# Ten instead of nine of the first table's sixteen column blocks on TensorE, and gathered rows of 768 instead of 896 columns

## The chip, the cores and the metric

The kernel runs on one core of one Trainium2 chip. The metric is the time of one execution on the device, in microseconds (us). Engines are named as in the profile: PE is TensorE's matmul side and PEld its weight load, DVE is VectorE, ACT is ScalarE, POOL is GpSimd and SP is SyncE, whose queue issues the plain loads here. The profile's source lines (L1879 and so on) are lines of the kernel file.

## What is computed

One layer of a decoder: an input projection, a recurrent (RWKV-7) and a sparse-attention mixer, an output projection, a layer norm, and then an expert mixer (PEER) with a second norm, for 256 prompt tokens and 32 sample tokens. The change concerns the expert mixer of the prompt tokens alone. Each token chooses 128 of 16384 experts (8 heads, 16 each). An expert e is a row of the first table, u, and a row of the second table, v, both 2048 wide:

```python
q = (xt @ wq).reshape(n, P_HEADS, 2, P_DKEY // 2)
s = jnp.einsum('nhcd,hckd->nhck', q, subkeys).astype(jnp.float32)
hv, hix = lax.top_k(s, P_TOPK)
...
tv, tpos = lax.top_k(cand, P_TOPK)
expert = jnp.take_along_axis(cand_e, tpos, axis=-1)
gate = jax.nn.softmax(tv, axis=-1).astype(x.dtype)
...
h = jax.nn.gelu(jnp.einsum('cd,chkd->chk', xb, u_tab[eb]), approximate=False)
return jnp.einsum('chk,chkd->cd', gb * h, v_tab[eb])
```

## The kernel before

**Two ways to one dot product.** For each token and chosen expert the kernel needs the dot product of the token with the expert's row of u, 2048 columns long, which is 16 column blocks of 128. The columns are split. The last NDB = 9 column blocks are computed densely on TensorE, for all 16384 experts and all 256 tokens, whether chosen or not. The first 7 blocks, UG = 896 columns, are computed sparsely: for one of a token's 128 choices, GpSimd gathers the 128 rows that 128 tokens chose (an indirect DMA of 128 x 896 floats, `gather` at L457), and VectorE multiplies them with the tokens and adds along the row (`dot`, L1803). There are 2 token tiles x 128 choices, so 256 such dots. Each writes one column of HD, and tile 0's 128 come first.

**The dense stage.** A loop over i1 from 0 to 127 (L1892) calls `dense` (L1874), which treats the 128 experts of one block:
- L1876 loads `ur`, 128 x 1152 floats (576 KB), over SP's queue into one of NUR = 3 buffers.
- L1879 multiplies the last three of the nine columns (NSP to NDB) in float32; such a matmul shows as two passes, so six passes a block. Xfd holds the tokens' part.
- The other NSP = 6 columns go in two halves, SPLIT = ((0, 3), (3, 6)). For a half, ACT casts the weights to f32r (`uh`, L1639), DVE subtracts the cast from the weights (`ul`, L1640), both in the helper `columns`, and PE makes three products a column: uh with XHd, uh with XLd, ul with XHd (L1886), nine passes a half, eighteen a block. uh and ul have three buffers each.
- L1888: ACT copies the block's sums from the PSUM bank `ph` (five banks) to AW, a store of all 16384 sums of each of 256 tokens.

After each block the loop puts ND or ND + 1 dots into VectorE's stream, by the rule `n_ = ND + (i1 * NDN % 8 < NDN)`: with ND = 1 and NDN = 4 it is 2, 1, 2, 1, so 1.5 a block. The gathers have a ring of NRW = 5 row buffers. Some dots already stand between the last selections ahead of the stage (the lines to L1431, with the helpers of `choose` and `settle`), beside the first blocks of `dense`. When tile 0's dots are done, `table(0)` (L1810) turns indices, gates and HD into TB.

**The weigh stage.** A loop over 68 steps (L1995 on) treats four tokens a step. `pick` (L1918) writes one-hot tables `oo` of the chosen indices on VectorE, PE transposes them (L1922, `pt`), ACT copies them (L1924, `oT`); PE multiplies them with AW (L1930, `px`); VectorE multiplies that with the other half of the one-hots and sums (L1941, `xj`, into E), which picks the dense sums of the chosen experts; then come the activation, the gate (L1949), the scaling (L1955) and a product that puts the weights back into AW (L1963, `pa`). These instructions are kept in the written order. The dots that are not done yet, `left` of them, are spread over the first 28 steps. From step 28 on the sample tokens' products follow (L1982, `fs`). `ws` (L1971) is one VectorE operation ahead of the loop.

**What sets the order.** The compiler's scheduler sorts the instructions of each engine by priorities; `tc.high_priority` lifts the casts and subtractions of the first NPRI = 12 blocks, and `issue_after` keeps an instruction behind another. On the chip each engine then takes its rows strictly in that order.

Behind the weigh stage the second table's products (L2058 and L2085) follow. The host arrays `in_peer_u_t` (dense part) and `in_peer_u_g` (gathered part) are cut by NDB and UG.

Of the kernel before, what the change touches and what calls it, by code (L numbers as in the profile page):

```python
# [11 lines left out]
F32R = mybir.dt.float32r  # L12
# [6 lines left out]
P = 128  # L19
# [30 lines left out]
NDW = 1  # L50
NPRI = 12
ND = 1
NDN = 4
NUR = 3
NRW = 5
NDB = 9
SPLIT = ((0, 3), (3, 6))
NSP = SPLIT[-1][1]
UG = 128 * (16 - NDB)
WF = 3  # L60
# [92 lines left out]
def hybrid_decode_step(ctx: ExitStack, tc: tile.TileContext, a, outs, dbg=None):  # L153
# [37 lines left out]
    def bank(tag="pb"):  # L191
        places = [(pool, nm, n) for _, div in psum for t_, pool, nm, n in div for _ in range(n) if t_ == tag]
        turn[tag] = k = (turn.get(tag, -1) + 1) % len(places)
        pool, nm, n = places[k]
        return pool.tile([P, 512], F32, name=tag, tag=nm, bufs=n)
# [1441 lines left out]
    def columns(pb, xh, xl):  # L1637

        sc.copy(xh, pb)  # L1639
        return ve.tensor_tensor(xl, pb, xh.bitcast(F32), OP.subtract)  # L1640
# [138 lines left out]
    dp, kc, kq = (Pool(nm, "left") for nm in ("dp", "kc", "kq"))  # L1779
    dp([P, NDB, P], "ur", bufs=NUR)  # L1780
    XHd, XLd = dp([P, NSP, NPR], "XHd", F32R), dp([P, NSP, NPR], "XLd", F32R)
    Xfd = dp([P, NDB - NSP, NPR], "Xfd")
    SKT = kq([P, 16, P], "SKT")
# [75 lines left out]
    for q in range(NSP // 2):  # L1859
        k2, x_ = slice(2 * q, 2 * q + 2), XT[:, 16 - NDB + 2 * q:18 - NDB + 2 * q, :]  # L1860
        sc.copy(XHd[:, k2, :], x_)
        gp.tensor_tensor(XLd[:, k2, :], x_, XHd[:, k2, :].bitcast(F32), OP.subtract)
    sc.copy(Xfd, XT[:, 16 - NDB + NSP:, :])
    xq.close()
# [8 lines left out]
    def dense(i1):  # L1873

        w = dp([P, NDB, P], "ur", bufs=NUR)
        sy.dma_start(w.rearrange("p k e -> p (k e)"), a["peer_u_t"][P * i1:P * i1 + P, :])  # L1876
        ph = bank("ph")
        for e in range(NSP, NDB):
            pe.matmul(ph[:, :NPR], w[:, e, :], Xfd[:, e - NSP, :], start=(e == NSP), stop=False)  # L1879
        for e0, e1 in SPLIT:  # L1880
            wh, wl = (dp([P, e1 - e0, P], nm, F32R, bufs=3) for nm in ("uh", "ul"))
            with tc.high_priority(offset=120 + 45 * i1 if i1 < NPRI else 0):
                lo_ = columns(w[:, e0:e1, :], wh, wl)
            for e in range(e0, e1):
                for wi, xi in ((wh, XHd), (wh, XLd), (wl, XHd)):
                    mm = pe.matmul(ph[:, :NPR], wi[:, e - e0, :], xi[:, e, :],  # L1886
                                   start=False, stop=(e == NSP - 1 and wi is wl))
        return lo_, mm, sc.copy(AW[:, i1 // 64, :, i1 % 64], ph[:, :NPR])  # L1888

    tabled = []  # L1890
    for i1 in range(P):
        lo_, mm, end = dense(i1)  # L1892
        n_ = ND + (i1 * NDN % 8 < NDN)
        with tc.issue_after(lo_.ins):
            dot(min(max(P - got[1], 0) or n_, n_))
        if got[1] >= P + 8 and not tabled:
            with tc.issue_after(mm.ins), tc.issue_after(end.ins):
                table(0)
            tabled.append(0)
# [168 lines left out]
    for k in range(P):  # L2068
# [12 lines left out]
        for t in range(2):  # L2081
            for wi, xi in ((ah, vh), (ah, vl), (al, vh)):
                for q in range(3):
                    n_ = min(512, FD - 512 * q)
# [9 lines left out]
        if 66 <= k < 114 and k % 6 == 0:  # L2094
            with tc.issue_after(ld_.ins):
                n_ = (k - 66) // 6
# [5 lines left out]
                else:  # L2102
                    t_, nm = ((g2_, "ln2_g"), (b2_, "ln2_b"))[n_ // 2 - 2]
# [67 lines left out]
```

## Time and profile before

| | us |
|---|---|
| median of 3 runs | 2496.15 (2490.72 to 2497.42) |
| the profiled execution | 2498.71 |
| its span | 2496.9 |
| dense stage, from the last selections to the last pass | 1243.1 to 1682.5 |
| weigh steps 0 to 27 | 1682.3 to 1815.6 |
| weigh steps 28 to 63 | 1815.6 to about 1940 |

A row of the profile's groups gives the line, the engine, the operation, the written tile, "<-" and the tiles that it reads, the shapes and the count; then the busy time and the mean duration in ns; then the idle time of the engine just ahead of these instructions, and what ended it. A row of a timeline has a start, a duration and, in square brackets, the wait ahead of it. The chain of waits follows the work that ended last from each step back to what released it. A row of windows gives, for a stretch of time, the busy time of each engine with its number of instructions, then the granted TensorE clock (1.00 is full speed), the DMA share and GB/s.

### The profile page before, as it was taken

How to read it: one execution, taken by the hardware profiler on the slowest of the kernel's cores; microseconds unless marked ns; L12 is line 12 of the kernel's file. 1: busy time of each engine (PE TensorE's matmuls, PEld its weight loads, DVE VectorE, ACT ScalarE, POOL GpSimd, SP SyncE). 2: the span in 40 equal slices, each digit the busy share in tenths (PEclk: the TensorE clock that was granted, in tenths of full speed). 3: DMA queues.
4: the chain of work that ended last, by engine and by line, in shares of the span. 5: the costliest groups of instructions: out<-in, count | busy, mean ns of one | idle time of the engine just before them, and what ended most of it. 6: DMA issues, size and time to landing. Idle time of an engine off the chain costs nothing.

```text
span 2496.9 us, 44823 instructions
## 1 busy us (share of the span) xinstructions
PE 2246.1 (90%) x16396; PEld 1888.6 (76%) x16396; DVE 1851.9 (74%) x4241; ACT 927.4 (37%) x1848; POOL 1373.4 (55%) x1422
## 2 busy tenths in 40 slices
PE   7979999988889997789699999996699799999996
PEld 7967898875545665678598889986676688888785
DVE  5789756554563446889977776779976799988888
ACT  4433222213441333220233343434566444443433
POOL 5677423242444005478655555556656488876662
PEclk9999999998896896899899999997899899999998
DMA  7777975457668884797499999996678599999995
GB/s 219 234 235 232 272 220 172 122 178 223 214 206 269 283 299 148 282 325 241 144 385 372 370 361 357 353 336 221 216 249 294 221 369 356 362 365 361 350 358 186
DMA packets 327613, 684.23 MB, mean 274 GB/s; under 512 B 82270, under 2 KB 200992, under 8 KB 326464
## 3 DMA queue, kind: packets, MB, share of 16 engines
q1 hardware_dynamic: 246176, 342.58, 41.4%
q0 software_dynamic: 81216, 338.78, 38.4%
q8 instruction: 129, 2.11, 0.3%
q14 instruction: 92, 0.75, 0.1%
HBM read 665.69 MB, written 23.88 MB: 276 GB/s over the span
## 4 chain that ended last, share of the span: by engine, by line
PE 60%; DVE 17%; DMA 8%; issue 7%; ACT 4%; POOL 3%; SPq 1%; DVEq 0%; POOLq 0%; ACTq 0%
PE pb L2085 17%; PE ph L1886 10%; PE pj L426 8%; PE ph L1879 3%; PE pa L1668 3%; PE p L1083 2%; DVE rows L1803 2%; DMA co<-in_cache_cmp_kv,gidx 2%; DVE sr L1559 2%; PE pa L1963 2%; DVE ul L1640 2%; PE ss L1500 1%; PE px L1930 1%; PE fs L1982 1%; DVE oo L1918 1%
## 5 line engine op out<-in xcount | busy, mean ns | idle before, releaser
L457 POOL DMA_INDIRECT rows<-in_peer_u_g,gi x256 | 332.3, 1298 | 239.5 <-DVE rows L1803 195.2
L457 POOL DMA_INDIRECT rq<-in_peer_v_g,gi x256 | 378.6, 1479 | 141.8 <-DVE fP L2058 80.2
L1803 DVE SCALAR_TENSOR_TENSOR rows<-rows,x1a 128x896 f32<-128x896 f32 x256 | 272.0, 1092 | 2.9 <-DMA rows<-in_peer_u_g,gi 2.7
L1886 PE MATMUL ph<-XHd,ul 128*128 128x256 f32 x768 | 225.3, 294 | 27.6 <-DVE ul L1640 22.7
L426 PE MATMUL pj<-XH,wl 128*128 128x288 f32 (+1 forms) x752 | 230.1, 306 | 15.2 <-DVE wl L421 9.1
L426 PE MATMUL pj<-XH,wh 128*128 128x288 f32 (+1 forms) x752 | 228.2, 304 | 13.6 <-DVE ss L756 6.9
L1886 PE MATMUL ph<-XHd,uh 128*128 128x256 f32 x768 | 236.7, 308 | 0.0
L2058 DVE SCALAR_TENSOR_TENSOR fP<-rq,ge,fP 128x640 f32<-128x640 f32 x254 | 223.8, 881 | 5.9 <-DMA rq<-in_peer_v_g,gi 3.4
L426 PE MATMUL pj<-XL,wh 128*128 128x288 f32 (+1 forms) x752 | 224.5, 299 | 0.0
L1640 DVE TENSOR_TENSOR ul<-ur,uh 128x384 fp32r<-128x384 f32 x256 | 131.8, 553 | 120.1 <-ACT uh L1639 93.3
L1886 PE MATMUL ph<-XLd,uh 128*128 128x256 f32 x768 | 217.4, 283 | 0.0
L2085 PE MATMUL pb<-vl,ah 128*128 128x512 f32 (+1 forms) x768 | 207.8, 378 | 1.4 <-issue 0.5
L2085 PE MATMUL pb<-vh,ah 128*128 128x512 f32 (+1 forms) x768 | 188.0, 380 | 20.9 <-ACT vh L2077 20.9
L2085 PE MATMUL pb<-vh,al 128*128 128x512 f32 (+1 forms) x768 | 205.7, 376 | 0.0
L419 ACT CAST wh<-wraw 128x512 fp32r<-128x512 f32 (+1 forms) x188 | 114.7, 617 | 223.7 <-PE pj L426 169.0
L1879 PE MATMUL ph<-Xfd,ur 128*128 128x256 f32 x768 | 187.6, 380 | 1.1 <-DMA ur<-in_peer_u_t 1.1
L1886 PEld LDWEIGHTS ph<-XHd,ul 128*128 128x128 f32 x768 | 147.0, 192 | 42.1 <-DVE ul L1640 41.8
L2085 PEld LDWEIGHTS pb<-vh,ah 128*128 128x128 f32 x768 | 145.5, 196 | 43.8 <-ACT vh L2077 24.5
L480 DVE SCALAR_TENSOR_TENSOR CA<-co,wbc,CA 128x256 f32<-128x256 f32 x248 | 133.9, 577 | 45.5 <-DMA co<-in_cache_cmp_kv,gidx 45.2
L2085 PEld LDWEIGHTS pb<-vl,ah 128*128 128x128 f32 x768 | 145.2, 195 | 24.5 <-DVE vl L2078 4.5
L426 PEld LDWEIGHTS pj<-XH,wl 128*128 128x128 f32 (+1 forms) x752 | 142.6, 190 | 26.6 <-DVE wl L421 12.7
L1888 ACT COPY AW<-ph 128x256 f32<-128x256 f32 x128 | 77.8, 608 | 228.1 <-PE ph L1886 198.7
(854 smaller groups left out, 5472.6 us busy)
## 6 DMA issues: line engine op xcount, KB each, us to landing
ur<-in_peer_u_t SPq DMA_DIRECT2D x128, 576.0 KB
wraw<-in_w_in SPq DMA_DIRECT2D x152, 256.0 KB
cw<-in_w_out SPq DMA_DIRECT2D x32, 512.0 KB
wraw<-in_w_out SPq DMA_DIRECT2D x32, 512.0 KB
wraw<-in_peer_wq SPq DMA_DIRECT2D x32, 512.0 KB
cw<-in_peer_wq SPq DMA_DIRECT2D x32, 512.0 KB
wraw<-in_w_in SPq DMA_DIRECT2D x64, 128.0 KB
co<-in_state_win_kv SPq DMA_DIRECT2D x16, 512.0 KB
```

The costliest lines, as they stand in the source:

```text
L419: sc.copy(wh[:, :, :n], w[:, :, :n])
L426: last[2] = pe.matmul(pb[:n, :nt], wi[:, k, :n], xi[(o + k) // 8][:, (o + k) % 8, :nt], start=(o + k == 0 and wi is wh and xi is xh), stop ...
L457: gp.indirect_dma_start(out=dst, out_offset=None, in_=rows_, in_offset=bass.IndirectOffsetOnAxis(ap=ix, axis=0))
L480: ve.scalar_tensor_tensor(d_, x_, w_, d_, op0=OP.mult, op1=OP.add)
L1640: return ve.tensor_tensor(xl, pb, xh.bitcast(F32), OP.subtract)
L1668: pe.matmul(acc[t], xi[:, e, P * t:P * t + P], wi[:, e, :], start=(k == e == n_ == 0), stop=(k == 6 and e == 1 and n_ == 2))
L1803: i_ = ve.scalar_tensor_tensor(r_, r_, 1.0, X1a[t], op0=OP.mult, op1=OP.mult, accum_out=h_)
L1879: pe.matmul(ph[:, :NPR], w[:, e, :], Xfd[:, e - NSP, :], start=(e == NSP), stop=False)
L1886: mm = pe.matmul(ph[:, :NPR], wi[:, e - e0, :], xi[:, e, :], start=False, stop=(e == NSP - 1 and wi is wl))
L1888: return lo_, mm, sc.copy(AW[:, i1 // 64, :, i1 % 64], ph[:, :NPR])
L2058: ve.scalar_tensor_tensor(fP[t], r_, w_, fP[t], op0=OP.mult, op1=OP.add)
L2085: pe.matmul(acc[3 * t + q][:, :n_], wi[:, P * t:P * t + P], xi[:, 512 * q:512 * q + n_], start=(k == 0 and wi is ah and xi is vh), stop=(k ...
```

## The change

One more column block of u is computed densely: NDB goes from 9 to 10. As six columns stay in f32r products, the float32 columns go from three to four (eight passes a block), `ur` grows to 640 KB a load, and Xfd to four columns. The sparse part shrinks to UG = 768 columns: the gathered rows are 3072 instead of 3584 bytes, and each dot is 768 long. NDN goes from 4 to 6, so the dots a block are 2, 1, 2, 2, which is 1.75 on the mean. `uh` gets two buffers instead of three, and `ul` keeps three.

```diff
@@ -50,10 +50,10 @@
 NDW = 1
 NPRI = 12
 ND = 1
-NDN = 4
+NDN = 6
 NUR = 3
 NRW = 5
-NDB = 9
+NDB = 10
 SPLIT = ((0, 3), (3, 6))
 NSP = SPLIT[-1][1]
 UG = 128 * (16 - NDB)
@@ -1878,7 +1878,7 @@
         for e in range(NSP, NDB):
             pe.matmul(ph[:, :NPR], w[:, e, :], Xfd[:, e - NSP, :], start=(e == NSP), stop=False)
         for e0, e1 in SPLIT:
-            wh, wl = (dp([P, e1 - e0, P], nm, F32R, bufs=3) for nm in ("uh", "ul"))
+            wh, wl = (dp([P, e1 - e0, P], nm, F32R, bufs=n_) for nm, n_ in (("uh", 2), ("ul", 3)))
             with tc.high_priority(offset=120 + 45 * i1 if i1 < NPRI else 0):
                 lo_ = columns(w[:, e0:e1, :], wh, wl)
             for e in range(e0, e1):
```

The change moves instructions in three places. The first is ScalarE late in the dense stage, from the casts of a few blocks up to the first copy of the weigh stage (`oT`). Before, the rows there are:

```order
L1639 CAST uh<-ur 128x384 x4
L1888 COPY AW<-ph 128x256 x2
L1639 CAST uh<-ur 128x384 x4
L1888 COPY AW<-ph 128x256 x2
L1924 COPY oT<-pt 128x512 x3
```

And with the change:

```order
L1639 CAST uh<-ur 128x384 x2
L1888 COPY AW<-ph 128x256
L1639 CAST uh<-ur 128x384 x2
L1888 COPY AW<-ph 128x256
L1639 CAST uh<-ur 128x384 x2
L1888 COPY AW<-ph 128x256 x2
L1924 COPY oT<-pt 128x512 x3
```

Two blocks' casts (four halves) and two blocks' copies stood together; now the two casts of one block and one copy alternate, the casts of a block ahead of the copy of the block ahead of it.

The second place is VectorE at the end of the dense stage and the first weigh steps: `ws` and the first two or three picks (`oo`), with the rows of tile 1's index table (`ii`) and the dots (`rows`). Before:

```order
L1640 TENSOR_TENSOR ul<-ur,uh 128x384 x2
L1803 SCALAR_TENSOR_TENSOR rows,hd_12151<-rows,x1a 128x896
L1971 TENSOR_TENSOR ws<-CT_61,ge_75 128x1024
L1918 TENSOR_TENSOR oo<-CT_61,TB 128x1024
L1803 SCALAR_TENSOR_TENSOR rows,hd_12151<-rows,x1a 128x896 x2
L1814 TENSOR_SCALAR ii<-gi_71 128x128
L1803 SCALAR_TENSOR_TENSOR rows,hd_12151<-rows,x1a 128x896
L1918 TENSOR_TENSOR oo<-CT_61,TB 128x1024
L1815 CAST ii<-ii 128x128
L1941 SCALAR_TENSOR_TENSOR xj,E<-px,oo 128x128 x4
```

And with the change:

```order
L1640 TENSOR_TENSOR ul<-ur,uh 128x384
L1803 SCALAR_TENSOR_TENSOR rows,hd_12151<-rows,x1a 128x768 x3
L1971 TENSOR_TENSOR ws<-CT_61,ge_75 128x1024
L1918 TENSOR_TENSOR oo<-CT_61,TB 128x1024
L1803 SCALAR_TENSOR_TENSOR rows,hd_12151<-rows,x1a 128x768
L1814 TENSOR_SCALAR ii<-gi_71 128x128
L1803 SCALAR_TENSOR_TENSOR rows,hd_12151<-rows,x1a 128x768 x2
L1815 CAST ii<-ii 128x128
L1803 SCALAR_TENSOR_TENSOR rows,hd_12151<-rows,x1a 128x768 x7
L1918 TENSOR_TENSOR oo<-CT_61,TB 128x1024
L1941 SCALAR_TENSOR_TENSOR xj,E<-px,oo 128x128 x4
```

Between the last subtraction and the second pick stand thirteen dots instead of four. Ahead of the first pick there are 218 of the 256 dots instead of 194; of the 38 left, ten stand between the first and the second pick, and 28 in the steps from there to step 27, where 59 stood between the same picks before.

The third place is VectorE among the last selections (L1420 makes indices out of the candidates, L1429 to L1431 the gates), just ahead of and behind the first index row of the table, L1814. Before:

```order
L1420 TENSOR_REDUCE EF<-rows 128x16
L1640 TENSOR_TENSOR ul<-ur,uh 128x384
L1429 TENSOR_REDUCE sm_13347<-ge_74 128x8
L1640 TENSOR_TENSOR ul<-ur,uh 128x384
L1803 SCALAR_TENSOR_TENSOR rows,hd_12150<-rows,x1a 128x896
L1640 TENSOR_TENSOR ul<-ur,uh 128x384
L1814 TENSOR_SCALAR ii<-gi_70 128x128
L1430 RECIPROCAL sm_13347<-sm_13347 128x8
```

And with the change:

```order
L1420 TENSOR_REDUCE EF<-rows 128x16
L1640 TENSOR_TENSOR ul<-ur,uh 128x384
L1431 TENSOR_TENSOR ge_74<-ge_74,sm_13347 128x128
L1803 SCALAR_TENSOR_TENSOR rows,hd_12150<-rows,x1a 128x768
L1640 TENSOR_TENSOR ul<-ur,uh 128x384
L1814 TENSOR_SCALAR ii<-gi_70 128x128
L1640 TENSOR_TENSOR ul<-ur,uh 128x384
L1815 CAST ii<-ii 128x128
```

Counted from the last selection on, five subtractions that stood ahead of L1814 now stand behind it. From step 28 of the weigh stage on, the rows of every engine are in the same order in both kernels.

## The prediction

> **What bounds the kernel now.** I read the page first, then the windows of the three stages that the edit touches, then the chain of waits and the timelines at their seams.
>
> ```profile
> span 2496.9 us, 44823 instructions
> PE 2246.1 (90%) x16396; PEld 1888.6 (76%) x16396; DVE 1851.9 (74%) x4241; ACT 927.4 (37%) x1848; POOL 1373.4 (55%) x1422
> 1243.10:1682.50 439.40, 434.42 (x2901) 397.10 (x2901) 316.29 (x635) 172.05 (x363) 248.29 (x194) 1.00 0.97 363
> 1682.50:1815.60 133.10, 90.02 (x531) 83.11 (x530) 128.01 (x395) 61.44 (x166) 81.81 (x62) 0.78 0.70 219
> 1815.60:1940.00 124.40, 122.65 (x954) 88.59 (x954) 86.83 (x352) 82.95 (x226) 69.69 (x61) 0.98 0.78 265
> ```
>
> A row of windows gives the length, then the busy time of PE, weight loads, DVE, ACT and POOL, the granted TensorE clock, the DMA share and GB/s. The averages of the page mix stages with different limits. The dense stage (1243 to 1682) is TensorE's: 434 of 439 us busy, while VectorE has 123 us free. The first 28 weigh steps (1682 to 1816) are VectorE's: 128 of 133 us busy, and TensorE waits. The weigh steps behind them (1816 to 1940) are TensorE's again. The edit takes dots from the second stage and gives columns to the first, so it trades VectorE time that counts for TensorE time that counts; the question is the rate.
>
> The chain inside the dense stage gives TensorE's prices and shows a gap.
>
> ```profile
> 1599.48 1.30 PE ph L1879 x6
> 1600.78 2.16 PE ph L1886 x18
> 1602.94 0.02 issue
> 1602.96 0.61 ACT AW L1888
> 1603.58 0.34 issue
> 1603.92 0.57 DVE ul L1640
> 1604.49 0.04 issue
> 1604.54 2.18 PE ph L1886 x16
> ```
>
> Six float32 passes (three columns) take 1.30 us, 0.217 each; eighteen f32r passes take 2.16, 0.120 each. A block is therefore 1.30 + 2.16 = 3.46 us. But here TensorE ended a block at 1602.94 and waited for AW's copy, the cast queued behind it and the subtraction. Over the stage, the 720 float32 passes of the window (quoted next) are 120 blocks, and 439.4 / 120 = 3.66 us: some 0.2 us a block, 22 us in all after 2 us of an odd block, are such gaps.
>
> ```profile
> L1879 PE MATMUL ph<-Xfd,ur 128*128 128x256 f32 x720 | 175.6, 379 | 0.8 <-DMA ur<-in_peer_u_t 0.7
> L1640 DVE TENSOR_TENSOR ul<-ur,uh 128x384 fp32r<-128x384 f32 x241 | 123.8, 554 | 120.1 <-ACT uh L1639 93.3 <-ACT AW L1888 26.6
> L1639 ACT CAST uh<-ur 128x384 fp32r<-128x384 f32 x240 | 112.7, 515 | 52.3 <-PE ph L1886 25.3 <-DMA ur<-in_peer_u_t 23.3 <-DVE rows L1803 2.2
> L1803 DVE SCALAR_TENSOR_TENSOR rows<-rows,x1a 128x896 f32<-128x896 f32 x192 | 203.3, 1085 | 1.8 <-DMA rows<-in_peer_u_g,gi 1.6
> ```
>
> The subtraction waits for casts, hardly ever for data, and the dots wait for rows 1.6 us in 192: VectorE has room, and so have the gathers.
>
> **Dense stage, one block.** A fourth float32 column adds two passes, 2 x 0.217 = 0.43 us: 8 x 0.217 + 18 x 0.120 = 3.89 us. The order of ScalarE's rows changes too: before, four casts, then two copies of AW; after, the two casts of a block always stand ahead of the copy of the block ahead of it. The gap above is thus removed. What is late next is a cast waiting for its uh buffer, of which there are two instead of three, one for each half block. The half frees when its products end; the other half, 1.08 us, and the next float32 passes, 1.73 us, follow before the new half is needed. Out of that 2.8 us go a cast and a subtraction (0.5 and 0.55 us): 1.7 us remain, more than one dot that may stand ahead of the subtraction. I cost the two buffers at nothing, and the cover is gone if a dot waits over about 0.8 us for its row. **So 128 blocks are 498.3 us of TensorE.**
>
> **Where it begins.** Some of it is done while the last selections still hold VectorE.
>
> ```profile
> L1879 PE MATMUL ph<-Xfd,ur x48: 377/379/625, 1190.0 to 1236.2; 128*128 128x256 f32 x48
> L1886 PE MATMUL ph<-XHd,uh x43: 277/283/472, 1191.1 to 1241.9; 128*128 128x256 f32 x43
> 1243.08 0.55 DVE L1640 TENSOR_TENSOR ul<-ur,uh 128x384 fp32r<-128x384 f32 x1
> 1243.55 0.22 DVE L1814 TENSOR_SCALAR ii<-gi 128x128 int32<-128x128 int32 x1
> 1694.79 1.08 DVE L1803 SCALAR_TENSOR_TENSOR rows<-rows,x1a 128x896 f32<-128x896 f32 x1
> 1695.80 1.09 DVE L1803 SCALAR_TENSOR_TENSOR rows<-rows,x1a 128x896 f32<-128x896 f32 x1
> 1184.57 1.21 DVE L1559 SCALAR_TENSOR_TENSOR sr<-sr,sx 128x1024 f32<-128x1024 f32 x1
> 1185.72 1.21 DVE L1559 SCALAR_TENSOR_TENSOR sr<-sr,sx 128x1024 f32<-128x1024 f32 x1
> ```
>
> (The counts are minimum, median and maximum ns, then the first and last start.) By 1243.1 TensorE had done 48 float32 passes and about 3 x 43 f32r passes, 25.9 us. The order moves five subtractions from ahead of L1814, the first index row of the table, to behind it; one costs VectorE 1243.55 - 1243.08 = 0.47 us. A dot: starts of 896 columns lie 1.01 us apart (1694.79 to 1695.80), of 1024 columns 1.15 (1184.57 to 1185.72). Through both, 768 columns are 0.88; the ends are 1.01 (no gain) and 0.80 (a price wholly proportional to columns would give 0.87, and I allow a little below). I take 0.88. Three dots ahead of L1814 save 0.4, so L1814 starts about 1243.55 - 2.35 - 0.4 = 1240.8. But by then nine half blocks are subtracted instead of fourteen: 81 f32r passes and 56 float32 passes, 21.9 us. 476.4 us remain, and with 4 us of waits (0 if every load is in time, 10 if the first blocks wait as they do before 1243) the stage ends at 1240.8 + 480.4 = **1721.2 instead of 1682.3: +38.9 us**, between +35 and +45.
>
> The cover of the added traffic: a block loads 640 instead of 576 KB and gathers 1.75 x 384 instead of 1.5 x 448 KB (both 672). That is 1.343 MB in 3.89 us, 345 GB/s; the window of before moved 363. No cost, down to a rate of 345.
>
> **The seam.** Behind the last subtraction the next picks (L1918, oo) wait for VectorE's queue.
>
> ```profile
> 1682.32 8.88 DMA rows<-in_peer_u_g,gi
> 1682.25 1.22 DVE L1918 TENSOR_TENSOR oo<-CT,TB 128x1024 f32<-128x1024 f32 x1
> 1686.56 1.22 DVE L1918 TENSOR_TENSOR oo<-CT,TB 128x1024 f32<-128x1024 f32 x1
> 1691.22 1.09 DVE L1803 SCALAR_TENSOR_TENSOR rows<-rows,x1a 128x896 f32<-128x896 f32 x1 [1.08 <-DMA rows<-in_peer_u_g,gi]
> 1682.32 1.98 POOL L457 DMA_INDIRECT rows<-in_peer_u_g,gi  x1 [0.30 <-issue]
> 1688.91 0.96 POOL L457 DMA_INDIRECT rows<-in_peer_u_g,gi  x1 [0.30 <-DVE xj L1941]
> 1682.47 0.60 ACT L1888 COPY AW<-ph 128x256 f32<-128x256 f32 x1 [2.82 <-PE ph L1886]
> ```
>
> Before, the second pick came 4.3 us after the last pass (1686.56). After, thirteen dots, ws and the first pick stand between the last subtraction, which ends some 2.4 us ahead of TensorE's end (0.84 for the products that need it and 1.6 of the slack above), and the second pick. As VectorE's own work this is 13 x 0.88 + 2 x 1.14 = 13.7, 11.3 us behind the end. Five rows lie ready at most; the other eight are gathered at 0.96 to 1.98 us each plus 0.30, and one here landed 8.9 us after its issue. If these set the pace it is 18 us. I take 14: **+9.7 us**, between +7 and +14.
>
> **The first 28 steps.** From the second pick to the 29th (number 28) are 27 steps.
>
> ```profile
> 1815.62 1.22 DVE L1918 TENSOR_TENSOR oo<-CT,TB 128x1024 f32<-128x1024 f32 x1
> 1826.99 0.59 PE pt L1922 x4
> 1827.58 0.89 PE pa L1963 x8
> 1828.47 0.99 PE px L1930 x8
> 1733.19 1.72 PE pa L1963 x8
> ```
>
> Before they took 1815.62 - 1686.56 = 129.06 us with 59 dots (by the order); less 59 x 1.01 a step is 2.57 without dots. That holds VectorE's waits, up to 0.19 a step by the 5.1 us of idle time in the window of this stage; I take 2.49 as its work. After the order has 28 dots there: 27 x 2.49 + 28 x 0.88 = 91.8 us, 3.40 a step, if VectorE alone sets it. TensorE's part of a step is 0.59 + 0.89 + 0.99 = 2.47 us at full clock, but L1963 took 1.72 at 1733. At a mean grant of 0.57, near the lowest that a stretch below shows, its part is 2.47 / 0.57 = 4.3 us a step, 116 us. The clock of the window above was 0.78 on the mean, and two dots less a step leave less slack against cold steps. I take 97, 5 above the floor: **-32 us**; bounds 92 and 116.
>
> ```profile
> 1767.40:1770.80 3.40, 2.55 (x13) 2.29 (x12) 3.26 (x13) 1.46 (x6) 2.52 (x2) 0.50 0.57 171
> 1774.20:1777.60 3.40, 2.42 (x20) 2.33 (x20) 3.30 (x13) 1.53 (x5) 2.62 (x2) 1.00 0.73 213
> ```
>
> In these two stretches TensorE is busy 2.55 and 2.42 us of 3.40, yet the grant is 0.50 in one and 1.00 in the other. [...]
>
> **The sum.** 1721.2 + 14 + 97 = 1832.2 for the 29th pick, against 1815.6: +16.6. From there on every engine's order is the same and TensorE sets the pace, so nothing is given back. The profiled execution took 2498.7 us (span 2496.9), which makes 2515.3; the median of the runs, 2496.15, lies 2.6 lower, so I forecast **2513 us**. A measurement of this kernel can tell about 0.3%, 7.5 us, from no change.
>
> **The rivals.**
> - *TensorE's clock sets the weigh steps* (0.12). If the mean grant falls from 0.78 to 0.57, the 27 steps take 116 instead of 97: 2532. For it, the stretches at 0.50; against it, shorter steps leave shorter pauses.
> - *The gaps stay* (0.08). If a row or the smaller uh ring holds the cast, 0.15 us over 120 blocks is +18: 2531. For it, the casts wait 52 us already, 25 of them for TensorE; against it, the 1.7 us of slack.
> - *Loads bind the dense stage* (0.05). At 330 GB/s a block is 4.07 us, +0.18 x 120 = +21: 2534. Against it, the 363 seen.
> - *Not slower: VectorE is the only limit from the last pass on* (0.15). No waits in the dense stage (1717.2), seam 11.3, steps 91.8: the 29th pick at 1820.3, +4.7, 2501. It needs rows to land as fast as VectorE takes them and cold steps to hide under the dots; from 9 us saved of the 12 between, the time is within 0.3%. With dots at 0.80 it would be 2498. Going below 2489 needs more than all floors together.
>
> My forecast (2504 to 2522) has 0.58; 0.02 is left for a gain I can't name. **Chances:** faster 0.05 (the lowest part of the last rival and the unnamed), same 0.17 (the rest of that rival and the forecast's lower edge), slower 0.78. The range takes in most of the last rival below and the clock and gap rivals above: 2497 to 2534.
>
> **What would show it.** In the profile of the changed kernel: float32 passes eight in a row and blocks 3.9 us apart with hardly any TensorE wait for ul (else the gap rival); the first table's index row near 1241; the last pass near 1721; a second pick 11 to 18 us behind it with row waits in front; some 3.6 us a step and a mean clock of 0.8 or more up to the 29th pick near 1832 (4.3 and 0.5 for the clock rival). The forecast is wrong if dense blocks are longer than 3.95 us, or if the later stages, which I hold the same, move.

## The result and the profile after

The changed kernel takes 2504.9 us at the median of 11 runs (2497.8 to 2515.3), the kernel before 2490.7 at the median of its 11 (2474.2 to 2498.0). The ratio is 1.0068, with a 95% interval of 1.0048 to 1.0088: slower by about 0.7%, 14.2 us between the medians where 17 were forecast. The 2504.9 lies inside the range forecast and 8.1 us below the 2513; 5.4 of those 8.1 are the kernel before, whose median was 2496.15 then and 2490.7 now. The profiled execution of the change took 2502.38 us, only 3.7 above that of before. The reason lies ahead of the change: TensorE's first product of the expert query (L1832) starts at a different time. In the timelines of before and of the change:

```profile
1063.27 17.10 PE L1832 MATMUL pj<-XT,wraw 128*128 128x256 f32 x78 [1.83 <-ACT XT L1744]
```

```profile
1050.79 17.53 PE L1832 MATMUL pj<-XT,wraw 128*128 128x256 f32 x80 [1.77 <-ACT XT L1744]
```

What stands ahead of it is untouched, yet it ended 12.5 us earlier. In the twelve profiles of this study the product starts between 1050.8 and 1075.5 us. So stages are compared from there: before has 2496.9 - 1063.3 = 1433.6 us left, the change 2500.6 - 1050.8 = 1449.8, **+16.2**.

The windows of the change, cut at its own seams (columns as before), with the row of its first table index and one of the pick that is the 29th:

```profile
span 2500.6 us, 45285 instructions
```

```profile
1227.30:1710.00 482.70, 479.94 (x3202) 452.61 (x3202) 321.19 (x684) 188.46 (x370) 223.18 (x215) 1.00 0.95 342
1710.00:1726.40 16.40, 3.44 (x15) 2.49 (x14) 11.92 (x25) 1.14 (x2) 12.86 (x11) 0.59 0.87 281
1726.40:1821.80 95.40, 68.50 (x515) 62.48 (x516) 89.46 (x328) 59.55 (x161) 46.06 (x29) 0.95 0.44 128
1821.80:1944.40 122.60, 121.47 (x958) 87.41 (x957) 86.89 (x356) 83.87 (x229) 69.44 (x60) 1.00 0.78 266
```

```profile
L1814 DVE TENSOR_SCALAR ii<-gi x4: 221/222/229, 1227.3 to 1713.0; 128x128 int32<-128x128 int32 x4
```

```profile
1821.76 1.22 DVE L1918 TENSOR_TENSOR oo<-CT,TB 128x1024 f32<-128x1024 f32 x1
```

| from, to | before | change | difference | forecast |
|---|---|---|---|---|
| first L1832, first L1814 | 180.3 | 176.6 | -3.7 | -2.8 |
| first L1814, last copy of AW | 438.9 | 482.6 | +43.7 | +41.6 |
| last copy of AW, second pick | 4.1 | 16.4 | +12.3 | +9.7 |
| second pick, 29th pick | 129.1 | 95.4 | -33.7 | -32 |
| 29th pick, end | 681.3 | 678.8 | -2.5 | 0 |
| sum (of unrounded numbers) | 1433.6 | 1449.8 | +16.2 | +16.6 |

The sum fits better than its terms do: two stages came out longer than forecast (by 2.1 and 2.6 us) and three shorter (by 0.9, 1.7 and 2.5), and these errors cancel to 0.4. That closeness is luck, the more so as the kernel before repeats within 3.6 us only (e9 below).

**The dense stage** is now one unbroken row of passes. The chain of the change:

```profile
1501.34 2.15 PE ph L1886 x18
1503.49 1.73 PE ph L1879 x8
1505.22 2.15 PE ph L1886 x18
1507.37 1.73 PE ph L1879 x8
```

1.73 + 2.15 is 3.88 us a block, as forecast from before's prices. The groups of the stage say why there is no gap:

```profile
L1886 PE MATMUL ph<-XHd,ul 128*128 128x256 f32 x741 | 209.3, 283 | 1.9 <-DVE ul L1640 1.9
L1640 DVE TENSOR_TENSOR ul<-ur,uh 128x384 fp32r<-128x384 f32 x247 | 137.5, 557 | 157.8 <-ACT uh L1639 157.8
L1639 ACT CAST uh<-ur 128x384 fp32r<-128x384 f32 x245 | 125.4, 513 | 285.7 <-PE ph L1886 282.2 <-DMA ur<-in_peer_u_t 3.5
```

The subtractions wait for casts and never for a copy of AW behind which a cast stands; the casts wait for TensorE, which frees their uh buffer; and TensorE waits 1.9 us in all for subtractions. ScalarE and VectorE follow TensorE now, instead of TensorE following them once in two blocks.

**The seam** is VectorE with ten dots and the pick (11.9 of its 16.4 us busy, in the window above), and in front of four of the dots waits for rows, 4.3 us in all. Three of these waits, in the timeline of the change, and the longer pieces of its chain there:

```profile
1715.49 0.99 DVE L1803 SCALAR_TENSOR_TENSOR rows<-rows,x1a 128x768 f32<-128x768 f32 x1 [1.37 <-DMA rows<-in_peer_u_g,gi]
1718.94 0.96 DVE L1803 SCALAR_TENSOR_TENSOR rows<-rows,x1a 128x768 f32<-128x768 f32 x1 [1.43 <-DMA rows<-in_peer_u_g,gi]
1725.48 0.96 DVE L1803 SCALAR_TENSOR_TENSOR rows<-rows,x1a 128x768 f32<-128x768 f32 x1 [1.20 <-DMA rows<-in_peer_u_g,gi]
1726.37 1.22 DVE L1918 TENSOR_TENSOR oo<-CT,TB 128x1024 f32<-128x1024 f32 x1
```

```profile
1708.47 6.93 DMA rows<-in_peer_u_g,gi
1716.76 0.80 POOL rows L457
1718.63 0.95 POOL rows L457
1720.17 5.22 DMA rows<-in_peer_u_g,gi
```

The chain goes through the landing of a row, a dot, two issues of GpSimd and the landing of another row: the rows set the pace, though VectorE, with its own work, is not far behind them. Meanwhile TensorE is busy for 3.4 of the 16.4 us.

**The steps** behind it take 3.53 us, and the chain of two of them no longer runs over VectorE alone (short pieces are left out):

```profile
1737.38 1.15 DVE oo L1918
1738.67 0.63 PE pt L1922 x4
1739.30 0.91 PE pa L1963 x8
1740.23 0.59 ACT AW L1964
1740.82 1.17 ACT oo L1955 x4
1742.53 0.31 DVE xj L1941 x2
1742.86 0.31 DVE xj L1941 x2
1743.55 0.74 issue
1744.37 1.15 DVE oo L1918
```

A turn from pick to transposes, product, copy, scaling and back takes two steps, 6.99 us, beside VectorE's own 2 x 3.40. That this turn sets the pace is read from the chain; no run shortens it.

### The profile page after: what moved, and what is told of

The parts are those of the page before. It is cut to its first block, busy times and chain, and to the rows that moved or that the text cites. A ratio compares the mean times of both kernels' runs of the same rounds, so it can differ in the third digit from the quotient of the medians.

```text
span 2500.6 us, 45285 instructions
## 1 busy us (share of the span) xinstructions
PE 2257.9 (90%) x16652; PEld 1921.1 (77%) x16652; DVE 1830.3 (73%) x4241; ACT 940.8 (38%) x1848; POOL 1330.6 (53%) x1422
## 3 DMA queue, kind: packets, MB, share of 16 engines
q8 instruction: 131, 2.15, 0.4%
## 4 chain that ended last, share of the span: by engine, by line
PE 67%; DVE 12%; DMA 9%; issue 5%; POOL 4%; ACT 3%; SPq 1%; DVEq 0%; POOLq 0%; ACTq 0%
PE pb L2085 19%; PE ph L1886 10%; PE ph L1879 8%; PE pj L426 7%; PE pa L1668 2%; PE p L1083 2%; PE pa L1963 2%; PE pj L1832 2%; PE px L1930 1%; PE ss L1500 1%; PE fs L1982 1%; DMA co<-in_cache_cmp_kv,gidx 1%; DMA co<-in_cache_sel_kv,sidx 1%; PE pt L1922 1%; DVE CA L480 1%
## 5 line engine op out<-in xcount | busy, mean ns | idle before, releaser
L457 POOL DMA_INDIRECT rows<-in_peer_u_g,gi x256 | 281.6, 1100 | 304.9 <-DVE rows L1803 282.8
L1640 DVE TENSOR_TENSOR ul<-ur,uh 128x384 fp32r<-128x384 f32 x256 | 142.2, 557 | 157.8 <-ACT uh L1639 157.8
L1803 DVE SCALAR_TENSOR_TENSOR rows<-rows,x1a 128x768 f32<-128x768 f32 x256 | 244.6, 961 | 8.2 <-DMA rows<-in_peer_u_g,gi 7.9
L1879 PE MATMUL ph<-Xfd,ur 128*128 128x256 f32 x1024 | 245.2, 382 | 4.5 <-DMA ur<-in_peer_u_t 4.5
L1639 ACT CAST uh<-ur 128x384 fp32r<-128x384 f32 x256 | 131.0, 513 | 310.0 <-PE ph L1886 291.0
L1886 PE MATMUL ph<-XHd,uh 128*128 128x256 f32 x768 | 241.7, 315 | 0.3 <-ACT uh L1639 0.3
L1886 PE MATMUL ph<-XHd,ul 128*128 128x256 f32 x768 | 218.2, 285 | 22.8 <-DVE ul L1640 22.8
L1886 PE MATMUL ph<-XLd,uh 128*128 128x256 f32 x768 | 217.6, 283 | 0.0
L1879 PEld LDWEIGHTS ph<-Xfd,ur 128*128 128x128 f32 x1024 | 186.9, 191 | 26.3 <-DMA ur<-in_peer_u_t 5.2
L1886 PEld LDWEIGHTS ph<-XHd,ul 128*128 128x128 f32 x768 | 147.1, 192 | 24.2 <-DVE ul L1640 24.0
```

The costliest lines, as they stand in the source:

```text
L457: gp.indirect_dma_start(out=dst, out_offset=None, in_=rows_, in_offset=bass.IndirectOffsetOnAxis(ap=ix, axis=0))
L1803: i_ = ve.scalar_tensor_tensor(r_, r_, 1.0, X1a[t], op0=OP.mult, op1=OP.mult, accum_out=h_)
L1886: mm = pe.matmul(ph[:, :NPR], wi[:, e - e0, :], xi[:, e, :], start=False, stop=(e == NSP - 1 and wi is wl))
```

## The experiments

Labels e1 to e10 are in the order of their running. Each time is compared by ratio with runs of the kernel before on the same chip, and each stage by the cuts of the table above; "behind the query" is the time from the first L1832 to the end (before 1433.6, change 1449.8). These stage times come from one profiled execution a kernel. Where an edit adds lines, the line numbers in its profile are shifted: in e1 the cast stands at L1886 and the products at L1890.

**e1: nine columns, casts put ahead of copies.** The gap of before was read from a chain; here it alone is removed. ScalarE's copy of a block is issued behind the casts of the next block, and the casts behind the copy before.

```diff
...
+                    if copied:
+                        behind.enter_context(tc.issue_after(copied[-1].ins))
+                    cast = sc.copy(wh, w[:, e0:e1, :])
...
-        return lo_, mm, sc.copy(AW[:, i1 // 64, :, i1 % 64], ph[:, :NPR])
+        summed.append((i1, ph))
+        if 12 <= i1 < P - 1:
+            with tc.issue_after(cast.ins):
+                while len(summed) > 1:
+                    end = store()
+                    copied.append(end)
```

> The kernel before, nine columns, with one thing forced: on ScalarE the two casts of a block stand ahead of the copy of the block ahead of it. Theory (the gaps of before come from that order alone): the gaps of 0.2 us a block go, a block takes 3.46 to 3.52 us, the dense stage shrinks from 439 us to 417 to 423, the seam and the 27 steps stay (4 and 129 us), and the time falls by 16 to 22 us. Rival (the loads bind, and the order only decides who is seen waiting): at 3.46 us a block the stage would need 369 GB/s where before moved 363, so the stage stays at 434 or more, TensorE now waits for ur, and the time stays within 5 us.

Measured: ratio 0.9924 (0.9899 to 0.9949). The windows of its dense stage and of its 27 steps, and its casts:

```profile
1237.00:1655.40 418.40, 417.30 (x2901) 396.94 (x2899) 322.05 (x633) 184.81 (x363) 240.06 (x193) 1.00 0.99 382
1658.60:1786.90 128.30, 86.89 (x518) 80.22 (x518) 123.97 (x391) 60.31 (x164) 78.26 (x60) 0.77 0.70 218
```

```profile
L1886 ACT CAST uh<-ur 128x384 fp32r<-128x384 f32 x240 | 116.4, 513 | 178.1 <-DMA ur<-in_peer_u_t 132.6 <-PE ph L1890 37.8 <-DVE rows L1803 6.5
```

The stage is 418.4 us instead of 438.9, 3.49 a block, and TensorE is busy in all but 1.1 us of it. The gaps were the order's. The casts now wait 133 us for loads, so the kernel stands at the edge of its loads, but at 382 GB/s, not at 363: the rate that the prediction took as the highest shown was no ceiling.

**e2: the change with 1.5 dots a block.**

```diff
-NDN = 6
+NDN = 4
```

> The changed kernel with the old number of dots a block (1.5): 62 dots again stand behind the first pick, three between the first two picks, 59 behind. Theory (VectorE's dots set the seam and most of the steps): the dense stage stays at 482 us, the seam shrinks from 16 to 4 or 5 us, the 27 steps grow from 95 to 27 x 2.49 + 59 x 0.88 = 119 (117 to 123), so the time is 10 to 14 us above the change's. Rival (in the steps TensorE's part sets the pace and dots are half hidden): the steps stay below 107 and the time is at or below the change's.

Measured: ratio 1.0361 (1.0328 to 1.0394), far outside both. Seam 3.9 us and steps 120.1 are as the theory has them (119), but the dense stage is 545.7. In its windows it begins normally and then breaks:

```profile
1300.00:1400.00 100.00, 99.56 (x663) 93.72 (x662) 60.00 (x125) 37.85 (x74) 42.80 (x39) 1.00 0.92 318
1400.00:1500.00 100.00, 86.13 (x546) 78.79 (x546) 49.69 (x106) 32.44 (x64) 35.44 (x31) 0.98 0.81 260
```

Its chain there goes from a subtraction to a load and waits for it:

```profile
1497.16 5.34 DMA ur<-in_peer_u_t
1502.51 0.04 issue
1502.55 1.99 PE ph L1879 x8
1504.54 2.38 PE ph L1886 x20
```

A load, 5.3 us, is issued only when a subtraction ends, and used at once. The order of TensorE's rows says why: from about block 44 on the scheduler let the float32 passes of a block slip ahead of products of earlier blocks, until at the end 45 products stand behind the last float32 passes instead of 18. A block's `ur` is then opened early and released late, and the ring of three has hardly any lead left: in this stage the float32 passes wait 45.8 us for `ur`, where in the change they wait 1.0.

**e3: nine columns with 1.75 dots a block.** In the kernel before:

```diff
-NDN = 4
+NDN = 6
```

> The kernel before, nine columns, with 1.75 dots a block: 205 instead of 194 dots ahead of the first pick, 23 between the first two, 28 behind. A block then moves 0.590 + 1.75 x 0.459 = 1.393 MB. Theory (gaps come from the order, loads do not bind up to 363 GB/s): at 363 GB/s a block takes 3.84 us, so the stage turns load-bound and grows to 450 to 462 us, the seam is 24 to 32 us, the steps 27 x 2.49 + 28 x 1.01 = 95; in all the time is within 10 us of before, not faster by more than 5. Rival (rows and loads have room to spare): the stage stays at 439 and the time falls by 8 to 12 us.

Measured: ratio 1.0036 (1.0015 to 1.0058). The time is as the theory has it, though not the way: the stage is 443.0 us and not 450, since it moved 370 GB/s, more than the 363 that the theory took for a limit, and since only 11 more dots than before were done ahead of the first pick; 23 were left to the seam, which is 37.2 us, above the 24 to 32 expected, with a wait for a row ahead of most dots.

```profile
1233.30:1676.30 443.00, 436.35 (x2901) 396.57 (x2899) 327.67 (x653) 170.03 (x363) 244.25 (x203) 1.00 0.98 370
1676.30:1713.50 37.20, 2.30 (x15) 1.64 (x14) 27.48 (x52) 1.14 (x2) 28.68 (x24) 0.56 0.87 302
```

In the second window GpSimd is busy 28.7 us and TensorE 2.3: rows set that seam, 37.2 / 23 = 1.6 us a dot, of which VectorE is busy 27.5 / 23 = 1.2.

**e4: the change with its dots held in place.** From block 20 on the subtractions are issued behind the dots of an earlier block, at last of the block just ahead:

```diff
...
+                    n_ = upto_.get(i1 - max(1, 6 - i1 // 20), 0)
+                    if i1 >= 20 and n_:
+                        behind.enter_context(tc.issue_after(dotted[n_ - 1].ins))
                     lo_ = columns(w[:, e0:e1, :], wh, wl)
```

> The changed kernel, in which from block 20 on the subtractions of a block are queued behind the dots of an earlier block, so that the dots do not fall behind: 226 instead of 218 stand ahead of the first pick, two instead of ten between the first two. Theory (the seam is made of dots that VectorE had room for in the dense stage): the seam falls from 16 to 4 to 8 us, the dense stage stays at 482 (to 486), the steps at 95, and the time falls by 7 to 12 us against the change's. Rival (the seam waits for something else, rows or the last copy of AW): it stays above 11 us. A third way: the queued subtractions reach TensorE late, and the stage grows by 5 us or more.

Measured: ratio 1.0031 (1.0012 to 1.0051), against 1.0068 of the change; some 9 us less by the ratios, which come from different chips, and 14.7 less behind the query (1435.1 us).

```profile
1229.70:1711.00 481.30, 478.49 (x3202) 451.40 (x3202) 332.00 (x701) 188.90 (x370) 248.65 (x225) 1.00 0.96 351
1711.00:1713.80 2.80, 1.01 (x7) 0.74 (x7) 2.80 (x6) 1.15 (x2) 2.48 (x2) 0.96 0.90 287
1713.80:1808.80 95.00, 67.93 (x525) 62.02 (x525) 89.68 (x328) 59.41 (x161) 46.00 (x29) 0.98 0.42 130
```

Eight dots moved into the dense stage cost nothing there, and the seam falls from 16.4 to 2.8 us. So the seam's +12.3 was no price of the tenth column, but of dots left over.

**e5: e2 with TensorE's order held.** The float32 passes are issued behind the last product (mm) of the block ahead:

```diff
...
+            if i1 >= 20:
+                behind.enter_context(tc.issue_after(summed[-1].ins))
...
+        summed.append(mm)
```

> The kernel of the run e2 (ten columns, 1.5 dots a block) with one more thing: from block 20 on the float32 passes of a block are queued on TensorE behind the last product of the block ahead of it, as they stand in the changed kernel. In e2 they slip a block ahead from block 44 on, and the ring of three loads waits. Theory (that slip made e2's dense stage 546 us long, and the dots only set seam and steps): the dense stage is 480 to 484 us, the seam 4, the steps 119 to 121, so that from the first query product to the end it takes 176 + 482 + 4 + 120 + 680 = 1462 us, 12 above the change's 1450, and the time is some 12 us above the change's. Rival (fewer dots or their gathers slow the loads in themselves): the dense stage stays above 510.

Measured: ratio 1.0114 (1.0077 to 1.0152); 1457.9 us behind the query, 8.1 above the change.

```profile
1232.00:1712.60 480.60, 478.11 (x3202) 451.29 (x3202) 307.44 (x637) 188.88 (x369) 212.85 (x193) 1.00 0.93 326
1715.40:1834.50 119.10, 75.04 (x518) 68.47 (x518) 115.87 (x390) 60.03 (x163) 73.84 (x61) 0.90 0.66 203
```

The dense stage is back at 480.6: e2's 65 us were the slip. The steps with 59 dots take 119.1 against 27 x 2.49 + 59 x 0.88 = 119.2, so with two dots a step VectorE alone sets them.

**e6: all dots in the dense stage.** The edits of e4 and e5 together, and two dots a block:

```diff
-NDN = 6
+NDN = 8
```

> The changed kernel with two dots a block, held in place on VectorE, and TensorE's order held as in e5: all 256 dots are done before the second pick. A block moves 0.655 + 2 x 0.393 = 1.442 MB. Theory (e1 has shown 382 GB/s, and a block of 3.88 us needs 372): the dense stage grows by less than 8 us to 481 to 489, the seam is 3 us, and the 27 steps without dots fall from 95 to 27 x 2.49 = 67 if VectorE sets them, or 70 to 80 if TensorE with its 2.47 us at full clock and the turn through the copies do; the time falls by 15 to 30 us below e4's. Rival (a step cannot go below some 3.4 us, as in the steps behind number 28, or the clock falls): steps stay at 88 or more and nothing is gained against e4.

Measured: ratio 1.0003 (0.9981 to 1.0024), on a chip where e4 was not run; 1436.1 us behind the query, e4's 1435.1 within a microsecond. The rival is right that nothing is gained against e4, but not why, and the theory's stage and steps are both off.

```profile
1242.50:1740.20 497.70, 485.63 (x3203) 455.15 (x3204) 360.95 (x762) 188.16 (x369) 292.27 (x255) 0.99 0.98 365
1739.60:1822.30 82.70, 68.22 (x537) 62.04 (x536) 65.38 (x271) 59.81 (x164) 0.00 (x0) 1.00 0.09 21
```

```profile
L1803 DVE SCALAR_TENSOR_TENSOR rows<-rows,x1a 128x768 f32<-128x768 f32 x253 | 236.8, 954 | 38.9 <-DMA rows<-in_peer_u_g,gi 35.2 <-issue 3.2
```

The steps without dots take 3.06 us (82.7 / 27), neither 2.49 nor 3.4: VectorE is busy 65 of 83 us and waits for the turn through TensorE and ScalarE (in the chain two steps, from the pick at 1785.75 to the one at 1791.86, are 6.11 us). But the dense stage grew by 16 us against e4. Dots there wait 35 us for rows (11 in e4), the queued subtractions with them, and TensorE waits 10.7 us for those (1.9 in e4).

**e7: e1 with 1.75 dots, held in place, and TensorE's order held.** The edits of e1, e4 and e5 on the kernel before, with nine columns and three uh buffers, and:

```diff
-NDN = 4
+NDN = 6
```

> The kernel of the run e1 (nine columns, casts ahead of copies) with 1.75 dots a block held in place on VectorE: 226 instead of 194 dots ahead of the first pick, 28 behind the second. A block moves 1.393 MB. Theory (loads bind at the 382 GB/s of e1): a block takes 3.65 us, the dense stage 418 + 0.16 x 120 = 438, the seam 3, the steps 98; in all 418 + 3 + 128 = 549 becomes 539, 5 to 12 us less than e1. Rival A (dots that go into a load-bound stage cost there what they save later): the dense stage is 448 or more and the time that of e1 or above. Rival B (the loads have more room): the stage stays below 428 and the time falls by 20 us or more.

Measured: ratio 0.9916 (0.9885 to 0.9947), which cannot be told from e1's 0.9924; the stage lies between the theory's 438 and rival A's 448.

```profile
1249.70:1694.30 444.60, 426.73 (x2901) 402.42 (x2899) 353.65 (x694) 180.11 (x362) 266.98 (x224) 0.98 1.00 392
1698.90:1797.10 98.20, 69.93 (x525) 64.27 (x524) 93.39 (x329) 59.49 (x161) 46.21 (x29) 0.96 0.46 141
```

The steps gain 30 us over e1 and the dense stage gives 26 of them back: at a DMA share of 1.00 and 392 GB/s TensorE is idle for 17.9 us of the stage (1.1 in e1), and over the whole execution the dots wait 40.9 us for rows and TensorE 33.7 us for subtractions. Beside e4, which has the tenth column, two uh buffers and other forced orders, it gives a rough price of that column where the dots are held in both: 1435.1 - 1405.7 = 29.4 us behind the query.

**e8: nine columns, uh in two buffers.** The change's third edit alone:

```diff
-            wh, wl = (dp([P, e1 - e0, P], nm, F32R, bufs=3) for nm in ("uh", "ul"))
+            wh, wl = (dp([P, e1 - e0, P], nm, F32R, bufs=n_) for nm, n_ in (("uh", 2), ("ul", 3)))
```

> The kernel before with one part of the change alone: uh in two buffers instead of three. The order of every engine stays as it was. Theory (the two buffers cost nothing and remove no gap): dense stage 439, seam 4, steps 129, time within 5 us of before. Rival (the third buffer's absence is what made casts and copies alternate, or it holds casts up): the stage is shorter or longer by 10 us or more.

Measured: ratio 1.0024 (0.9997 to 1.0050). The stage is 445.9 us against 438.9, and 1442.3 us behind the query, 8.7 more than before; both lie between the theory and the rival.

```profile
1257.70:1703.60 445.90, 438.73 (x2927) 401.45 (x2926) 319.12 (x638) 172.91 (x365) 254.80 (x194) 1.00 0.97 360
```

The two buffers alone did not remove the gaps: late in the stage ScalarE still has four casts, then two copies (52 such groups, 47 before). But the orders are not quite those of before. Ahead of the first L1814, TensorE had done 43 float32 and 108 f32r passes instead of 50 and 128, which at 0.217 and 0.120 us is some 3.9 us left over for the stage. Whether the buffers cost anything beyond that the interval leaves open.

What made casts and copies alternate can be read from e2, which differs from e8 in NDB alone: with ten columns, ScalarE's rows alternate in e2 as in the change, though its dots are those of before. So the step from nine to ten columns (with its shorter rows) is enough for the better order, with two uh buffers and at 1.5 dots a block. No run has ten columns and the old order.

**e9 and e10: both kernels once more,** with no edit.

> The kernel before once more, unchanged, for its profile. Theory (what lies ahead of the first query product, L1832, varies from run to run by some 25 us in kernels that are alike there, and what lies behind it does not): from the first query product to the end 1432 to 1437 us as in the first profile (1433.6), dense stage 437 to 441, steps 128 to 130, wherever the product itself starts between 1050 and 1076. Rival (the first profile of before was an unusual one behind that point too): the part behind differs by 6 us or more.

> The changed kernel once more, unchanged, for its profile. Theory: from the first query product to the end 1448 to 1452 us (1449.8 in the first profile), dense stage 481 to 485, seam 15 to 18, steps 94 to 97, so the change costs 14 to 18 us behind that point, as the two first profiles say. Rival: the part behind varies as the part ahead does, by 10 us or more, and the 16 us are partly chance.

Measured: 1430.0 and 1449.9 us behind the query; ratios 0.9987 (0.9964 to 1.0009) and 1.0075 (1.0040 to 1.0111). Dense stages 439.7 and 480.7, seams 4.1 and 15.5, steps 128.7 and 97.6. The change repeats within 0.1 us there and before within 3.6, slightly more than expected, so the change costs 16 to 20 us there. By the medians it is 14.2 us in the first comparison and 18.2 between e9 and e10. The queries began at 1059.0 and 1057.7.

## Why the prediction was right, point by point

- *TensorE's prices* (0.217 and 0.120 a pass, 3.89 a block): 3.88 measured, and the stage at +43.7 for +41.6. The 4 us of waits put on top were about right: TensorE idles 2.8 us in the window of the stage.
- *Where the stage begins*: the first L1814 comes 3.7 us earlier in the first pair and 2.4 in the second (178.9 and 176.5 us behind the query), for the 2.8 forecast, though six subtractions fewer stand ahead of it in the traces (10 instead of 16) and not five. By then TensorE had done 48 float32 passes and not 56, which leaves 8 x 0.217 = 1.7 us more to the stage, most of its 2.1 above the forecast.
- *The gaps go because casts stand ahead of copies*: shown by e1, in which that alone takes 20.5 us out of the stage of the kernel before; the prediction had read 22 us of gaps. This is the largest thing that the change got for nothing, and it was read from the orders of the two kernels, not foreseen from the edit: the tenth column's own work is 0.43 x 128 = 55 us, of which the stage shows 43.7.
- *Two uh buffers at nothing*: with ten columns TensorE waits 1.9 us for subtractions, so it holds there; e8 leaves it open for nine.
- *No cost of the loads up to 345 GB/s*: right for the change (342), but the 363 behind it were a demand, not a limit; e1 and e7 moved 382 and 392. The load rival's 330 GB/s was seen as a limit nowhere.
- *The seam*, taken at 14, measured 16.4 and 15.5, within its bounds 11.3 to 18. It was mis-sized by about 2 us towards VectorE's own 11.3; the chain runs through rows, as in e3 with its 1.6 us a dot.
- *The steps*, taken at 97, measured 95.4 and 97.6, between VectorE's 91.8 and the clock rival's 116. Only a small part of the rest above the floor is a lower clock (0.95 and 0.90 granted, 0.78 before): in e4, at 0.98, the steps are 95.0 all the same, 3.2 above the floor. The turn through ScalarE that the chain shows, 3.50 a step, fits the rest. The prediction named less slack against steps at a low clock as the reason and did not have this turn. The floor price of 2.49 and 0.88 holds where VectorE sets the steps: e5 hits 119.2 by 119.1. Without dots it does not (3.06 in e6).
- *Nothing behind the 29th pick*: -2.5 in the first pair; the second pair has 678.6 and 679.5, so nothing is clearly given back or won there.
- *The rival on the other side* fell at its first condition: rows did not land as fast as VectorE takes them. e4 shows how near it was: with eight of the ten dots out of the seam the kernel is at 1.0031.

Of the clock the traces show this much. In the seam of the change:

```profile
1712.29 0.65 PE L1922 MATMUL pt<-CT,oo 128*128 128x128 f32 x4 [2.27 <-DVE oo L1918]
1713.62 2.07 PE L1930 MATMUL px<-AW,oT 128*128 128x128 f32 x8 [0.68 <-ACT oT L1924]
1727.64 1.12 PE L1922 MATMUL pt<-CT,oo 128*128 128x128 f32 x4 [10.26 <-DVE oo L1918]
1712.90:1717.30 4.40, 2.73 (x11) 2.07 (x10) 3.03 (x9) 0.59 (x1) 3.48 (x4) 0.50 0.90 307
```

The longest pause behind the dense stage was 2.27 us when eight passes of px took 2.07 us at a grant of 0.50; the pause of 10.26 us came only later. The first steps of the kernel before:

```profile
1684.86 1.16 PE L1930 MATMUL px<-AW,oT 128*128 128x128 f32 x8 [0.68 <-ACT oT L1924]
1687.83 1.11 PE L1922 MATMUL pt<-CT,oo 128*128 128x128 f32 x4 [1.82 <-DVE oo L1918]
1689.62 2.08 PE L1930 MATMUL px<-AW,oT 128*128 128x128 f32 x8 [0.25 <-ACT oT L1924]
1684.86:1686.10 1.24, 1.15 (x8) 0.96 (x8) 1.24 (x4) 0.00 (x0) 1.24 (x1) 1.00 1.01 381
1689.60:1691.70 2.10, 2.08 (x8) 1.78 (x8) 1.01 (x3) 0.00 (x0) 1.22 (x2) 0.50 0.91 280
```

There eight passes of px took 1.16 us at a grant of 1.00 and, one step later, 2.08 at 0.50; the longest pause behind the dense stage had been 1.82 us by then, and in all of these steps none is above 3.32 us. What lowers the grant, and what brings it back, no run here settles.

## What to carry to other kernels

A trade between two engines is priced at the stage where each of them is the bound: here a column costs TensorE 0.43 us a block where TensorE has nothing to spare, and saves VectorE dots of which part would have fitted into idle time anyway. Before trading, look whether the stage that pays has gaps of its own: putting a block's casts ahead of the copy behind them gave 0.76% in the kernel before, as much as the whole trade cost (0.68%). And read the order that the scheduler makes of each variant: a change of one count let passes slip a block ahead, took the lead from a ring of three loads, and cost 65 us that had nothing to do with that count's own price.

## What the runs showed of the hardware that was not expected

One core moved 392 GB/s of loads and gathered rows over 445 us at a DMA share of 1.00. A run of 23 gathers back to back (e3) came to 1.6 us for each 128 rows of 896 floats, where VectorE's dot needs 1.01. TensorE's granted clock was 0.50 when the longest pause behind the dense stage had been 1.82 us (the second step of the kernel before). And work that is alike in all kernels, ahead of the query, ended anywhere in a band of 25 us (1050.8 to 1075.5) from run to run, more than the change itself costs, while behind that point the changed kernel repeated within 0.1 us.
